# Building half of the MLP's low weight parts with an accumulating DMA instead of a VectorE subtraction

## The chip, the core and the metric

The kernel runs on one NeuronCore of a Trainium2 chip. Five instruction streams matter here: PE (TensorE: matrix products into PSUM), DVE (VectorE), ACT (ScalarE), POOL (GpSimd, here only the issuer of a few DMAs) and SP (SyncE, the issuer of nearly all DMAs). Each stream runs its own instructions in order and waits on semaphores for the others. Transfers between HBM and SBUF are done by 16 DMA engines that serve all queues.

The metric is the device time of one execution in microseconds (us). The kernel before takes 2251.57 us, the median of three runs (2249.9 to 2251.72).

## What is computed

A two-layer decoder trunk over 256 positions with a model width of 2048, in float32. Layer 0 mixes positions with two recurrent head groups, layer 1 with a dilated sliding-window attention. Each layer ends with the same MLP, whose hidden width is 8192:

```python
def squared_relu_mlp(h, w1, w2):
    return jnp.square(jax.nn.relu(h @ w1)) @ w2

def reference(...):
    h = x
    for layer in range(DEPTH):
        hn = rms_norm(h, norm_mix[layer])
        ...
        h = h + mix
        h = h + squared_relu_mlp(rms_norm(h, norm_mlp[layer]), mlp_w1[layer], mlp_w2[layer])
    return rms_norm(h, final_norm)
```

The change touches only the weights `mlp_w1` (2048 x 8192 in each layer) and `mlp_w2` (8192 x 2048 in each layer), which are 256 MB of the kernel's float32 weights.

## The kernel before

**Products from two parts.** The kernel gives PE its operands as `F32R`. Every operand is split into a high part, its value rounded by the cast to that type, and a low part, what the rounding left over: `w = hi + lo`. A product is then the sum of three: high by high, high by low and low by high. The activations are kept split in `bufa` and `bufb`, with the high halves in columns 0 to 255 and the low halves in columns 256 to 511 of each block.

**Weight tiles ("units").** All weights are cut into units of 128 x 2048 values, 1 MB each. They are listed in the order of use in `units`; the MLP's are 256 of them. In each layer four rounds `q` follow one another, each with 16 units of `w1` and then 16 units of `w2`. `unit()` hands out the split unit that is due and calls `fetch()` for one that is due later. `fetch()` takes a buffer `raw` (three exist), issues the load on SP and constructs `Weights`, which splits the unit in two halves of 1024 columns:

- `A.copy(h, w)` at L97: ACT rounds the raw half into `hi`.
- `V.tensor_tensor(l, w, h, subtract)` at L98: DVE writes `lo = raw - hi`.

The pools `whi` and `wlo` hold five half tiles each, so two and a half units. Half number n (counted over all units) therefore takes the place of half n - 5, and can be written only when PE has used that one for the last time.

**How PE uses a unit of `w1`.** `project` with `cross` goes through 16 blocks of 128 columns, and for each issues one product with `hi` (512 columns wide) and one with `lo` (256 wide). The first half tile is free in the middle of the unit and the second at its end. The result goes from PSUM through `folded` (ACT copies at L182, DVE adds at L184), DVE's squared ReLU (L571) and `split_to` (ACT L189, DVE L190) into `bufb`.

**How PE uses a unit of `w2`.** `tokens` goes twice through the unit, once for each half of the positions (`j`), with four blocks `i` of 512 columns each time and three products in a block: (xh, hi), (xh, lo), (xl, hi). Blocks 0 and 1 lie in the first half tile and 2 and 3 in the second. The first half tile is thus free after six of the eight steps and the second after all eight. `add_res` (DVE L536) adds the result to the residual.

**What sets the order.** All products go through `mm`, which chains them in program order. The rest is ordered by a scheduler that sees priorities: weight loading and splitting run ahead (`stream`), and short evacuations further ahead (`urgent`). Once scheduled, the order on each engine is fixed. POOL issues three small DMAs: two tables at the start (L207, L209) and the positions at L596.

Of the kernel before, what the change touches and what calls it, by code (L numbers as in the profile page):

```python
# [10 lines left out]
F32 = mybir.dt.float32  # L11
# [3 lines left out]
AF = mybir.ActivationFunctionType  # L15
OP = mybir.AluOpType
# [24 lines left out]
def trunk_kernel(ctx, tc, x, xtok, cols, tab, masks, pos, fin, w_in, w_gate, w_out, w_qkv, w_o, w1, w2, out):  # L41
    nc = tc.nc
# [13 lines left out]
    V, A, T = nc.vector, nc.scalar, nc.tensor  # L56
# [8 lines left out]
    made = {}  # L65
# [6 lines left out]
    for step in ORDER.split():  # L72
        src, first, n = where[step[0]]
# [9 lines left out]
    at = [0, 0]  # L83

    class Weights:
        def __init__(self, raw, now=True):
            self.raw = raw
            self.hi = [whi.tile([P, 1024], F32R, name="hi") for _ in range(2)]
            self.lo = [wlo.tile([P, 1024], F32R, name="lo") for _ in range(2)]
            if now:  # L90
                self.split(0, 1024)
                self.split(1024, 1024)

        def split(self, at, n):
            h, l = self.part(at, n)
            w = self.raw[:, at:at + n]
            A.copy(h, w)  # L97
            V.tensor_tensor(l, w, h.bitcast(F32), OP.subtract)  # L98

        def part(self, at, n):  # L100
            i, r = divmod(at, 1024)
# [2 lines left out]
    def fetch():  # L104
        u = at[0]
        if u >= len(units):
            return
        at[0] += 1
        src, i = units[u]
        with stream():  # L110
            r = wraw.tile([P, 2048], F32, name="raw")
            nc.sync.dma_start(r, src[i])
            made[u] = Weights(r)

    def fetch_first():
        for u in range(4):
# [18 lines left out]
    def unit(src, i):  # L135
        u = at[1]
        assert units[u][0] is src and units[u][1] == i, (u, i)
        at[1] += 1
        if u + 2 >= at[0]:
            fetch()  # L140
        return made.pop(u)
# [379 lines left out]
    for step in ORDER.split():  # L521
        i = int(step[1])
# [173 lines left out]
    r = tmp.tile([P, 2], F32, name="nr2", bufs=2)  # L696
# [6 lines left out]
    for h in range(2):  # L703
        at = slice(h * 1024, h * 1024 + 1024)
# [111 lines left out]
```

## Time and profile before

The profile shows one execution. Its span, from the first to the last instruction, is 2248.2 us; the same execution took 2250.34 us as timed, so 2.1 us lie around the span. Line numbers are those of the kernel before.

| what | value |
|---|---|
| time, median of three runs | 2251.57 us |
| time of the profiled execution | 2250.34 us |
| its span | 2248.2 us |
| granted TensorE clock, share of full | 0.998 |
| DVE busy | 1411.2 us (63%) |
| ACT busy | 1059.7 us (47%) |
| POOL busy | 1.9 us |
| read from HBM | 410.70 MB |

"Busy" is the time in which an engine executes an instruction. A group of instructions is given as line, engine, operation and tiles, followed by count, total busy time and mean duration. "Idle before" is the time for which the engine stood still just ahead of these instructions, with the one whose semaphore ended it. The DMA share is the mean busy share of the 16 DMA engines. The time of a DMA to landing runs from its issue to the arrival of its last byte's semaphore.

### The profile page before, as it was taken

The page shows a single profiled execution, that of the slowest core. Times are in us where ns is not written, and L with a number is a line of the kernel's source. Part 1 is how long each engine was busy: PE and PEld are TensorE (multiplying, and loading weights), DVE is VectorE, ACT ScalarE, POOL GpSimd, SP SyncE. Part 2 cuts the span into 40 slices and gives each one's busy share as a digit, 9 for nine tenths or more (in the row PEclk, how much of TensorE's full clock was granted, in tenths as well). Part 3 has the DMA queues.
Part 4 walks back from the last instruction along what each step waited for, and adds up shares of the span by engine and source line. Part 5 has one row for each costly group of instructions (what it writes and reads, how often), then busy time and mean ns, then how long its engine had stood idle before and what let it go on. Part 6 is the DMA issues. An engine that isn't in the chain of part 4 may idle for free.

```text
span 2248.2 us, 30488 instructions
## 1 busy us (share of the span) xinstructions
PE 2228.6 (99%) x12196; PEld 1930.5 (86%) x12196; DVE 1411.2 (63%) x2212; ACT 1059.7 (47%) x1537; POOL 1.9 (0%) x7
## 2 busy tenths in 40 slices
PE   9999999999999999999999999999999999999997
PEld 8999998888888888888888888888888888888886
DVE  7777896565565565565567878556655655655654
ACT  6444585444344344344545445454434444434443
POOL 0000000000000000000000000000000000000000
PEclk9999999999999999999999999999999999999999
DMA  8444445555555555555554554555555555555553
GB/s 307 151 161 160 150 167 190 187 188 187 199 185 182 201 187 187 187 190 185 187 189 168 171 185 169 187 186 181 178 198 193 188 187 191 185 188 204 188 185 114
DMA packets 58717, 414.51 MB, mean 184 GB/s; under 512 B 6528, under 2 KB 7296, under 8 KB 9168
## 3 DMA queue, kind: packets, MB, share of 16 engines
q1 hardware_dynamic: 58320, 412.20, 52.0%
q8 instruction: 95, 1.56, 0.3%
q0 software_dynamic: 256, 0.38, 0.1%
q14 instruction: 46, 0.38, 0.0%
HBM read 410.70 MB, written 2.10 MB: 184 GB/s over the span
## 4 chain that ended last, share of the span: by engine, by line
PE 97%; ACT 1%; DVE 1%; issue 0%; DMA 0%; SPq 0%; ACTq 0%; DVEq 0%
PE p L146 94%; PE pl L423 1%; PE pl L548 0%; ACT hi L97 0%; PE pl L646 0%; DMA raw<-in_w_in 0%; PE po L667 0%; PE pd L659 0%; DVE bufa L193 0%; ACT L158 0%; DVE lo L98 0%; PE pd L407 0%; PE pl L645 0%; ACT gi L158 0%; PE po L668 0%
## 5 line engine op out<-in xcount | busy, mean ns | idle before, releaser
L98 DVE TENSOR_TENSOR lo<-raw,hi 128x1024 fp32r<-128x1024 f32 (+1 forms) x774 | 945.0, 1221 | 733.4 <-ACT hi L97 717.2
L97 ACT CAST hi<-raw 128x1024 fp32r<-128x1024 f32 (+1 forms) x774 | 811.2, 1049 | 1004.3 <-PE p L146 809.7
L146 PE MATMUL p<-bufa,hi 128*128 128x512 f32 (+1 forms) x3840 | 1147.2, 361 | 2.6 <-DVE bufa L193 2.6
L146 PE MATMUL p<-bufa,lo 128*128 128x256 f32 x3200 | 902.4, 282 | 0.0
L146 PE MATMUL p<-hi,bufb 128*128 128x512 f32 x2560 | 793.7, 390 | 0.0
L146 PEld LDWEIGHTS p<-bufa,hi 128*128 128x128 f32 x3840 | 681.4, 189 | 119.6 <-DVE bufa L193 3.8
L146 PEld LDWEIGHTS p<-bufa,lo 128*128 128x128 f32 x3200 | 605.8, 189 | 1.1
L146 PEld LDWEIGHTS p<-hi,bufb 128*128 128x128 f32 x2560 | 479.9, 188 | 99.1
L146 PE MATMUL p<-lo,bufb 128*128 128x512 f32 x1280 | 498.2, 389 | 0.0
L146 PEld LDWEIGHTS p<-lo,bufb 128*128 128x128 f32 x1280 | 240.3, 188 | 49.5
L146 PE MATMUL p<-hi,bufa 128*128 128x512 f32 x384 | 123.1, 396 | 0.7 <-ACT hi L97 0.6
L146 PEld LDWEIGHTS p<-hi,bufa 128*128 128x128 f32 x384 | 71.7, 188 | 16.1 <-ACT hi L97 1.6
L146 PE MATMUL p<-lo,bufa 128*128 128x512 f32 x192 | 76.2, 397 | 1.8 <-DVE lo L98 1.8
L189 ACT CAST bufb<-z 128x256 fp32r<-128x256 f32 x136 | 54.3, 399 | 17.4 <-DVE z L571 14.5
L536 DVE SCALAR_TENSOR_TENSOR xall<-p,nm,xall 128x512 f32<-128x512 f32 x64 | 47.9, 748 | 20.1 <-PE p L146 20.1
L190 DVE TENSOR_TENSOR bufb<-z,bufb 128x256 fp32r<-128x256 f32 x136 | 57.0, 419 | 3.8 <-ACT bufb L189 3.8
L571 DVE SCALAR_TENSOR_TENSOR z<-z 128x256 f32<-128x256 f32 x128 | 54.5, 426 | 4.4
L184 DVE TENSOR_TENSOR z<-p,t 128x256 f32<-128x256 f32 x128 | 53.5, 418 | 0.0
L182 ACT COPY t<-p 128x256 f32<-128x256 f32 x128 | 46.9, 366 | 0.0
L247 ACT ACTIVATE z<-xall 128x512 bf16<-128x512 f32 x32 | 20.2, 632 | 55.7 <-DVE xall L536 55.7
L146 PEld LDWEIGHTS p<-lo,bufa 128*128 128x128 f32 x192 | 36.1, 188 | 10.7 <-DVE lo L98 3.7
L423 PE MATMUL pl<-qk 128*128 128x64 f32 x224 | 31.1, 261 | 0.0
(197 smaller groups left out, 730.6 us busy)
## 6 DMA issues: line engine op xcount, KB each, us to landing
raw<-in_w SPq DMA_DIRECT2D x256, 1024.0 KB, 4.8
raw<-in_w_qkv SPq DMA_DIRECT2D x48, 1024.0 KB, 4.8
raw<-in_w_in SPq DMA_DIRECT2D x46, 1024.0 KB, 4.8
raw<-in_w_out SPq DMA_DIRECT2D x16, 1024.0 KB, 4.7
raw<-in_w_o SPq DMA_DIRECT2D x16, 1024.0 KB, 4.8
xall<-in_xtok SPq DMA_DIRECT2D x1, 2048.0 KB, 9.2
raw<-in_w_gate SPq DMA_DIRECT2D x2, 1024.0 KB, 4.8
out<-xall SPq DMA_DIRECT2D x4, 512.0 KB, 4.0
```

The source lines that it names most:

```text
L97: A.copy(h, w)
L98: V.tensor_tensor(l, w, h.bitcast(F32), OP.subtract)
L146: chain[:] = [after(T.matmul(*args, **kw), chain)]
L182: A.copy(t, p[:, S:])
L184: V.tensor_tensor(z, p[:, :S], t, OP.add)
L189: A.copy(dst[:, :S], src)
L190: V.tensor_tensor(dst[:, S:], src, dst[:, :S].bitcast(F32), OP.subtract)
L247: A.activation(q, xres[:, j, n * 512:n * 512 + 512], AF.Square, accum_out=self.ss[:, j, n:n + 1])
L423: T.matmul(pl[:, j], kq[:, js], halves(qp[:, js], c, True), start=True, stop=True)
L536: V.scalar_tensor_tensor(xres[:, j, at], ps[j], 1.0 if scale is None else scale[:, j:j + 1], xres[:, j, at], op0=OP.mult, op1=OP.add)
L571: V.scalar_tensor_tensor(z, z, 0.0, z, op0=OP.max, op1=OP.mult)
```

## The change

Units of the MLP with an odd index no longer use DVE for their low part. ACT writes the negated high part into `lo`, and a DMA issued by POOL then reads the same weights from HBM a second time and adds them onto `lo`, so that `lo = -hi + raw`. Even units, and all units of other weights, keep the subtraction on DVE. In the changed kernel the subtraction stands at L100, the high part at L98, the negation at L102 and the accumulating DMA at L103.

```diff
     class Weights:
-        def __init__(self, raw, now=True):
+        def __init__(self, raw, now=True, again=None):
             self.raw = raw
+            self.again = again
...
             w = self.raw[:, at:at + n]
             A.copy(h, w)
-            V.tensor_tensor(l, w, h.bitcast(F32), OP.subtract)
+            if self.again is None:
+                V.tensor_tensor(l, w, h.bitcast(F32), OP.subtract)
+            else:
+                A.activation(l, h.bitcast(F32), AF.Copy, scale=-1.0)
+                nc.gpsimd.dma_start(l, self.again[:, at:at + n], accum_op=OP.add)
...
             r = wraw.tile([P, 2048], F32, name="raw")
             nc.sync.dma_start(r, src[i])
-            made[u] = Weights(r)
+            made[u] = Weights(r, again=src[i] if src in (w1, w2) and i % 2 else None)
```

There are 128 such units, 64 of `w1` and 64 of `w2`, with two halves each: 256 instructions move from DVE to ACT, and 256 DMAs of 128 x 1024 float32 (512 KB) are new on POOL's queue. The order of PE's instructions stays as it was but for five groups of four transposes (L548), which move ahead by a few products. In the `w1` stage ACT's fixed order for two units becomes: `t`, negation, `bufb`, high part, negation, high part, `t`, high part, `bufb`, high part. In the `w2` stage it is: high part, negation, high part, negation, high part, high part.

## The prediction

> **What bounds the kernel now.** I read the page first: the busy shares and the chain that ended last.
>
> ```profile
> span 2248.2 us, 30488 instructions
> ...
> PE 2228.6 (99%) x12196; PEld 1930.5 (86%) x12196; DVE 1411.2 (63%) x2212; ACT 1059.7 (47%) x1537; POOL 1.9 (0%) x7
> ...
> PE 97%; ACT 1%; DVE 1%; issue 0%; DMA 0%; SPq 0%; ACTq 0%; DVEq 0%
> ```
>
> PE is never without work for long: 19.6 us of 2248.2. The waits of PE alone say who is to blame for what is left.
>
> ```profile
> PE p L146 <- DVE bufa L193: 2.6, 4, 0.9
> PE p L146 <- DVE lo L98: 1.8, 4, 0.8
> PE po L447 <- ACT st L433: 1.3, 1, 1.3
> PE po L202 <- DVE spare L577: 1.1, 1, 1.1
> PE p L146 <- ACT hi L97: 0.6, 1, 0.6
> ```
>
> The columns are total us, times, longest. All DVE waits together are 2.6 + 1.8 + 1.1 = 5.5 us. The low part made by DVE, which the change wants to relieve, holds PE up for 1.8 us in the whole execution. The stretch of layer 0's MLP, taken by itself, has no hole at all (busy us of PE, PEld, DVE, ACT, POOL; then clock, DMA share, GB/s):
>
> ```profile
> 432.75:1074.08 641.33, 641.33 (x3283) 546.08 (x3284) 370.74 (x450) 281.52 (x363) 0.00 (x0) 1.00 0.54 189
> ```
>
> So the MLP runs at PE's pace at full clock, DVE is busy 58% of it, and the DMA engines 54%. The change can win next to nothing. What it can lose depends on whether the new, longer way to `lo` still fits in the lead that the five half tiles give.
>
> **What is removed.** 256 of DVE's 774 subtractions go, and ACT gets as many negations.
>
> ```profile
> L98 DVE TENSOR_TENSOR lo<-raw,hi 128x1024 fp32r<-128x1024 f32 (+1 forms) x774 | 945.0, 1221 | 733.4 <-ACT hi L97 717.2
> ```
>
> DVE loses 256 x 1.221 = 313 us, none of it on the path that sets the end except at most the 1.8 us above. I count nothing for it.
>
> **What is added on ACT.** The nearest rows are the rounding copy of the same size, and an activation and a copy of 128x256.
>
> ```profile
> L97 ACT CAST hi<-raw 128x1024 fp32r<-128x1024 f32 x770 | 808.8, 1051 | 1003.3 <-PE p L146 809.7 <-issue 187.9 <-DVE hz L635 4.7
> L189 ACT CAST bufb<-z 128x256 fp32r<-128x256 f32 x136 | 54.3, 399 | 17.4 <-DVE z L571 14.5 <-DVE z L517 2.8
> L182 ACT COPY t<-p 128x256 f32<-128x256 f32 x128 | 46.9, 366 | 0.0
> ...
> L158 ACT ACTIVATE qk<-hz 128x256 f32<-128x256 f32 x16 | 6.5, 409 | 0.0
> ```
>
> An activation costs 409 - 399 = 10 ns more than a cast, so a negation is 1.06 us and all of them 271 us. ACT then has for two `w1` units 4 x 1.05 + 2 x 1.06 + 2 x (0.40 + 0.37) = 7.9 us. To know what that is out of, the pace of a unit is needed, from ACT's timeline in a `w1` stage:
>
> ```profile
> 860.94 1.05 ACT L97 CAST hi<-raw 128x1024 fp32r<-128x1024 f32 x1 [1.51 <-issue]
> 861.89 0.37 ACT L182 COPY t<-p 128x256 f32<-128x256 f32 x1
> 863.73 1.05 ACT L97 CAST hi<-raw 128x1024 fp32r<-128x1024 f32 x1 [1.47 <-PE p L146]
> 864.68 0.40 ACT L189 CAST bufb<-z 128x256 fp32r<-128x256 f32 x1
> 866.60 1.05 ACT L97 CAST hi<-raw 128x1024 fp32r<-128x1024 f32 x1 [1.51 <-issue]
> ```
>
> From 860.94 to 866.60 a unit takes 5.66 us, two take 11.3, and ACT fills 7.9 of these. Work that queues behind a negation (`t` and `bufb`, for which DVE's ReLU and, after three PSUM buffers, PE wait) comes up to 1.06 us later; three buffers are two units of cover. Where the cover is thin, at the end of a layer with its short chain of ACT and DVE steps, eight groups late by 1.06 us would cost 8.5 us. I count nothing.
>
> **What is added on the way to `lo`.** Before: place free, high part 1.05, subtraction 1.22. Now: place free, high part, negation, DMA, semaphore. Call L the time from the DMA's issue to its landing. How large may L be? In the `w2` stage ACT's timeline shows when places come free:
>
> ```profile
> 1059.43 1.05 ACT L97 CAST hi<-raw 128x1024 fp32r<-128x1024 f32 x1 [3.04 <-PE p L146]
> 1060.78 1.05 ACT L97 CAST hi<-raw 128x1024 fp32r<-128x1024 f32 x1 [0.30 <-PE p L146]
> 1064.87 1.05 ACT L97 CAST hi<-raw 128x1024 fp32r<-128x1024 f32 x1 [3.04 <-PE p L146]
> ```
>
> A `w2` unit takes 1064.87 - 1059.43 = 5.44 us, and the two frees are 1.35 us apart, which is two of the eight steps, as the loop says. The second half of an odd unit takes the place of the first half of the unit two before (n - 5 is 2u + 1 - 5). That one is free at 6/8 of its unit and the new one is needed at 2/8 of its own: 1.5 x 5.44 = 8.16 us, and 0.23 more because a product with `hi` goes first (24 in 5.44 us). Off go 1.05 and 1.06 on ACT and some 0.1 for semaphores: **L may be 6.2 us**. The first half has 2 units, 10.88 us, and so L up to 8.9. In `w1` a first half has 11.3 + 0.24 (two thirds of a block's 5.66 / 16), less 0.95 for the high part until `t` starts (861.89 - 860.94), 0.37 and 1.06: L up to 9.1; the second half has about the same, since `bufb` ahead of it is done by the time its place is free.
>
> And how large is L? No accumulating DMA is in this trace. The rows for DMAs (KB each, median us to landing):
>
> ```profile
> raw<-in_w SPq DMA_DIRECT2D x256, 1024.0 KB, 4.8
> ...
> tab__187<-in_tab POOLq DMA_DIRECT2D x1, 257.0 KB, 3.8
> ...
> ppi<-in_pos POOLq DMA_DIRECT2D x1, 32.0 KB, 2.0
> ```
>
> From 32 KB to 1024 KB it is 2.8 us more, so 2.9 us per MB on top of a fixed 1.9. An accumulation has to read its target as well as its source: 512 KB written need 1024 KB read. One pass over 512 KB would be 1.9 + 1.45 = 3.4 us, two passes 4.8, if the DMA engines are free. They are not: the raw loads fill 54% of them, so in the mean the moving part stretches by 1/(1 - 0.54) = 2.17: one pass 5.0, two passes 1.9 + 2.9 x 2.17 = 8.2. The other bound is the table row: from 32 to 257 KB it takes 1.8 us more, 8.0 us per 1000 KB, from POOL's queue in the crowded start; its fixed part is then 1.7, and two passes at that price are 1.7 + 8.2 = 9.9. **L lies between 3.4 and 9.9. I take 8.2**: the price of the raw loads, which fill the same stretch, with two passes, since a read of the target can't be left out. Then the second half of each odd `w2` unit is 8.2 - 6.2 = 2.0 us late. PE waits for it, frees the places later, and the next round starts as much later: the loss repeats for each of 2 x 4 x 8 = 64 units. In `w1`, 8.2 is below 9.1, but the engines' own time is short there: per two units 2 MB of raw loads and two passes over 1 MB are 4 x 2.9 = 11.6 us, in 11.3. That is 0.3 us for each of 64 pairs. (In `w2` the same 11.6 fits in 10.9 + 2.0.)
>
> The row of the raw loads says nothing of a second operand. The Trainium skill, Collectives: The Full Stack, "The bandwidth ceiling: the fold count and why AG ≠ RS ≠ AR", says that an adding DMA runs at about half the rate of a copy (measured 1.93) because it needs two source reads. By that factor L would be about 8.0 us, 1 MB of accumulation 5.6, and the time an estimated 2250 + 64 x 1.8 + 64 x 0.1 = 2372 us; by the bare row with one pass L is 5.0, and the time unchanged. No run so far shows which holds.
>
> **What is queued on POOL.** The 256 DMAs stand behind the positions' DMA, which waits for layer 0's mixers, and in order among themselves.
>
> ```profile
> POOL ppi L596 <- PE po L449: 297.8, 1, 297.8
> ```
>
> That wait ends about 300 us in, ahead of the first MLP unit, so it delays nothing. SP's loads of `raw` start no later than before: an odd unit's `raw` is free after ACT alone.
>
> **The sum.** 64 x 2.0 + 64 x 0.3 = 147 us on the profiled execution's own 2250.3: 2397. Against the median (2251.57) it would be 2399; I state 2397.
>
> **The rivals.**
>
> *Hidden, no slower.* The raw load and the accumulation fall in different parts of a unit's time, so that they hardly share: L is 4.8 to 6.2, below the limit in both stages. For it: the DMA engines idle 46% of the MLP, and `w2`'s limit is missed by only 2.0. Against it: the sharing has to be avoided 64 times. The time stays at 2250, with the DVE waits gone 2244.8 at best. It decides from L below 6.2. The Trainium skill, DMA: Bandwidth & Descriptors, "Anatomy of one DMA — SWDGE (gpsimd) path", gives about 2.0 us plus the bytes at 436 GB/s for a DMA from POOL's queue; that estimate is 3.2 us for one pass and 4.4 for two, which lands here.
>
> *The DMA engines become the bound.* If 1 MB of accumulation costs over 7.1 us (a late `w2` pair, 10.9 + 2.0, less 5.8 of raw loads), every pair of units, in `w1` and in `w2`, takes what the DMA engines take. At the table row's 8.2 us per MB in one pass a pair is 5.8 + 8.2 = 14.0, so 64 x (2.7 + 3.1) = 371 us more: 2621; in two passes 22.2, and 3671. For it: that row is the only large one from POOL's queue, and the price of the adding itself is unknown. Against it: the table was loaded among the crowded first loads.
>
> *DVE holds POOL up.* If POOL can't write a DMA's descriptors while DVE works, each waits up to one subtraction, 1.22 us. L is 9.4, `w2` loses 3.2 x 64 = 205, `w1` 0.3 x 64 = 19: 2474. Against it: DVE's instructions become fewer. The Trainium skill, SBUF — State Buffer, "Who interferes with whom", says that a DVE instruction in a two-port mode shuts GpSimd out for its whole length, and that a `tensor_tensor` has no such mode and gets in the way of GpSimd's reads only; no run so far shows either.
>
> *Only ACT's delay shows.* L fits, and the ends of the layers cost the 8.5 us of above: 2259.
>
> **How the numbers follow.** The forecast, late low parts in `w2`, with L from just over 6.2 to some 9.5 (3.3 x 64 + 0.4 x 64 = 237, so 2256 to about 2490): 0.45. DMA engines as the bound: 0.28. Hidden: 0.17. DVE holding POOL: 0.05. ACT's delay alone: 0.05. A measurement of this kernel tells 0.2%, 4.5 us, from no change: three runs lie within 1.8 us. Of the hidden case 0.03 is faster and 0.14 the same; all others are slower, 0.83. The range runs from 2249, which takes in the hidden case, to 2850: half of the DMA-bound case lies above it (0.14) and the 0.03 below, so 0.83 is inside. The forecast's own range is 2256 to 2490.
>
> **What would show it.** The accumulating DMAs' row with about 8 us to landing; PE's waits in `w2`, on products with `lo`, of about 2 us at each odd unit, and of some 0.3 us in `w1`; DMA share in the MLP of 0.9 and more; the negation at 1.06 us. If PE waits in `w1` as long as in `w2` and the DMA share is near 1, the DMA engines are the bound. If PE has no new wait, L is below 6.2 and the forecast is wrong.

## The result, and the profile after

| | before | changed |
|---|---|---|
| time, median | 2251.49 us (four runs, 2249.9 to 2251.72) | 2417.94 us (four runs, 2402.99 to 2434.6) |
| ratio | | 1.0743, 95% interval 1.0704 to 1.0782 |
| span of the profiled execution | 2248.2 us | 2401.2 us |
| mean granted TensorE clock | 0.998 | 0.992 |

The kernel became 7.4% slower; 2397 us had been forecast. The profiled execution is the fastest of the four. The page of the changed kernel, its busy shares, the DMA engines' share by slices, POOL's DMA queue, the chain that ended last and the DMA issues:

```profile
PE 2269.8 (95%) x12196; PEld 1935.6 (81%) x12196; DVE 1114.3 (46%) x1956; ACT 1320.8 (55%) x1793; POOL 222.7 (9%) x263
...
DMA  8444455999999999999855454579999989999996
...
q0 software_dynamic: 37120, 134.61, 31.4%
...
PE 51%; DMA 30%; issue 17%; ACT 1%; POOL 1%; DVE 0%; POOLq 0%; SPq 0%; ACTq 0%; DVEq 0%
...
raw<-in_w SPq DMA_DIRECT2D x256, 1024.0 KB, 6.6
lo<-in_w POOLq DMA_DIRECT2D x256, 512.0 KB, 7.6
```

The two MLP stretches stand out in the DMA row: where the engines were half busy they are now at nine tenths and more. The new DMAs on POOL's queue took 31.4% of all engines' time, 754 us for 128 MB, so 5.9 us per MB written. The chain that ended last, 97% PE before, now leads for 30% through DMAs, nearly all of them these. DVE lost 297 us of busy time and ACT gained 261; in the chain ACT has 1%, as before, and DVE nothing.

PE's waits, and the groups of its products with `lo` (busy us and mean ns, then idle time just before and what ended it):

```profile
PE p L151 <- DMA lo<-in_w: 111.3, 95, 3.2
PE p L151 <- DVE bufa L198: 2.5, 4, 0.8
PE p L151 <- DVE lo L100: 1.6, 3, 0.8
```

```profile
L151 PE MATMUL p<-bufa,lo 128*128 128x256 f32 x3200 | 907.7, 284 | 26.4 <-DMA lo<-in_w 25.6
...
L151 PE MATMUL p<-lo,bufb 128*128 128x512 f32 x1280 | 511.4, 400 | 85.8 <-DMA lo<-in_w 85.7
...
L103 POOL DMA_DIRECT2D lo<-in_w x256 | 220.7, 862 | 1858.5 <-ACT lo L102 1824.6
...
L102 ACT ACTIVATE lo<-hi 128x1024 fp32r<-128x1024 f32 x256 | 271.3, 1060 | 6.0
```

One wait is new and it is the accumulating DMA: 25.6 us of it ahead of `w1`'s products (in from `bufa`), 85.7 ahead of `w2`'s (in from `bufb`). The other two rows are nearly as they were. The old wait for DVE's low part was 1.8 us; it went down to 1.6, which is all that relieving DVE brought.

Here is one such wait, from the timelines of POOL and PE in a `w2` stage:

```profile
966.18 0.86 POOL L103 DMA_DIRECT2D lo<-in_w  x1 [5.94 <-ACT lo L102]
971.10 0.86 POOL L103 DMA_DIRECT2D lo<-in_w  x1 [4.06 <-ACT lo L102]
```

```profile
976.39 0.61 PE L151 MATMUL p<-hi,bufb 128*128 128x512 f32 x2
979.04 0.50 PE L151 MATMUL p<-lo,bufb 128*128 128x512 f32 x1 [2.04 <-DMA lo<-in_w]
979.38 0.72 PE L151 MATMUL p<-hi,bufb 128*128 128x512 f32 x2
979.90 0.63 PE L151 MATMUL p<-lo,bufb 128*128 128x512 f32 x1
980.33 1.05 PE L151 MATMUL p<-hi,bufb 128*128 128x512 f32 x2
```

The second half's DMA is issued at 971.10. PE has done the products with `hi` at about 977.0 and starts the first with `lo` at 979.04, 7.9 us after the issue. Then something happens that was not in the forecast: a product with `lo` takes 0.63 us instead of 0.39. The stretches around it show why (busy us of PE, PEld, DVE, ACT, POOL; then granted clock, DMA share, GB/s):

```profile
820.00:912.00 92.00, 89.43 (x498) 76.16 (x497) 36.80 (x62) 58.27 (x78) 13.78 (x16) 1.00 1.00 266
912.00:1010.00 98.00, 90.10 (x383) 71.88 (x382) 25.01 (x26) 50.15 (x49) 13.62 (x16) 0.98 0.94 253
976.00:979.80 3.80, 1.76 (x8) 1.17 (x7) 0.41 (x1) 1.57 (x2) 0.87 (x1) 1.00 0.90 237
979.80:983.20 3.40, 3.40 (x9) 2.63 (x9) 0.75 (x1) 0.00 (x0) 0.00 (x0) 0.50 1.03 235
983.20:987.00 3.80, 3.80 (x18) 3.09 (x18) 1.18 (x2) 3.05 (x3) 0.86 (x1) 1.00 0.45 111
```

The first row is a `w1` stage with the DMA engines fully busy, the second the `w2` stage behind it. The third holds the wait, and in the 3.4 us after it the granted clock is 0.50. There are nine such stretches of 3.4 us in this execution's MLPs, none before. They are the step from 0.998 to 0.992 in the mean clock: 0.006 x 2401 = 14 us. The other executions of the changed kernel had 0.990, 0.985 and 0.983, and the four times rise as the clock falls, from 2402.99 to 2434.6 us. So the clock's part differs from run to run and is larger in the median than in the profile.

### The profile page after: what moved, and what is told of

The parts are those of the page before. It is cut to its first block, busy times and chain, and to the rows that moved or that the text cites. A ratio compares the mean times of both kernels' runs of the same rounds, so it can differ in the third digit from the quotient of the medians.

```text
span 2401.2 us, 31090 instructions
## 1 busy us (share of the span) xinstructions
PE 2269.8 (95%) x12196; PEld 1935.6 (81%) x12196; DVE 1114.3 (46%) x1956; ACT 1320.8 (55%) x1793; POOL 222.7 (9%) x263
## 3 DMA queue, kind: packets, MB, share of 16 engines
q0 software_dynamic: 37120, 134.61, 31.4%
## 4 chain that ended last, share of the span: by engine, by line
PE 51%; DMA 30%; issue 17%; ACT 1%; POOL 1%; DVE 0%; POOLq 0%; SPq 0%; ACTq 0%; DVEq 0%
PE p L151 48%; DMA lo<-in_w 29%; POOL lo L103 1%; PE pl L428 1%; ACT hi L98 0%; PE pl L553 0%; PE pl L651 0%; DMA xall<-in_x 0%; PE po L672 0%; PE pd L664 0%; ACT L163 0%; PE pd L412 0%; PE pl L650 0%; ACT gi L163 0%; PE po L673 0%
## 5 line engine op out<-in xcount | busy, mean ns | idle before, releaser
L98 ACT CAST hi<-raw 128x1024 fp32r<-128x1024 f32 (+1 forms) x774 | 810.0, 1047 | 891.1 <-PE p L151 873.0
L100 DVE TENSOR_TENSOR lo<-raw,hi 128x1024 fp32r<-128x1024 f32 (+1 forms) x518 | 631.1, 1219 | 876.8 <-ACT hi L98 871.9
L151 PE MATMUL p<-bufa,lo 128*128 128x256 f32 x3200 | 907.7, 284 | 26.4 <-DMA lo<-in_w 25.6
L151 PE MATMUL p<-hi,bufb 128*128 128x512 f32 x2560 | 803.4, 394 | 0.0
L151 PE MATMUL p<-lo,bufb 128*128 128x512 f32 x1280 | 511.4, 400 | 85.8 <-DMA lo<-in_w 85.7
L151 PEld LDWEIGHTS p<-hi,bufb 128*128 128x128 f32 x2560 | 486.1, 190 | 100.6
L103 POOL DMA_DIRECT2D lo<-in_w x256 | 220.7, 862 | 1858.5 <-ACT lo L102 1824.6
L102 ACT ACTIVATE lo<-hi 128x1024 fp32r<-128x1024 f32 x256 | 271.3, 1060 | 6.0
```

The lines of the kernel that those rows point to most:

```text
L102: A.activation(l, h.bitcast(F32), AF.Copy, scale=-1.0)
L103: nc.gpsimd.dma_start(l, self.again[:, at:at + n], accum_op=OP.add)
L151: chain[:] = [after(T.matmul(*args, **kw), chain)]
```

## The experiments

The theory after the result: the accumulation costs the DMA engines about twice what a copy of as many bytes costs, lands later for it, and PE waits wherever the time to landing is above what the place's lead allows: 6.2 us for a second half in `w2`, about 9 elsewhere. The rivals were ACT's negations, the second read from HBM, POOL's path, and DMA time alone without any lead. Every experiment is an edit of the changed kernel, except one of the kernel before. Times are medians, each beside its own runs of the kernel before (2251.56 to 2251.64 us).

**The DMA copies and does not add** (`x1_copy`).

```diff
-                nc.gpsimd.dma_start(l, self.again[:, at:at + n], accum_op=OP.add)
+                nc.gpsimd.dma_start(l, self.again[:, at:at + n])
```

> The DMA from GpSimd stays, with its wait for the negation and its second read of the weights, but it overwrites lo and does not add (lo = raw, so the output is not the reference's). Theory (the second operand doubles the DMA engines' time: a 4096-byte piece of the accumulation takes 328 ns, a plain one about 160): time to landing falls from 7.6 to about 5 us, below w2's limit of 6.2, and the kernel takes 2250 to 2262 us. Rival (the second read from HBM, or GpSimd's path, costs the time whatever the DMA does): no change, 2390 to 2430 us.

2302.47 us, ratio 1.0228 (1.0209 to 1.0246). The time lies in neither range: two thirds of the loss go, but not all. The price did fall. The page's queue row and issue row of this run:

```profile
q0 software_dynamic: 37120, 134.61, 19.1%
...
lo<-in_w POOLq DMA_DIRECT2D x256, 512.0 KB, 5.8
```

19.1% of 2296.6 us is 439 us for 128 MB, 3.4 us per MB against 5.9. A piece of 4096 bytes takes 174 ns in the median of the packet records and 328 with the addition. But in `w2` the second halves still landed 6.4 us after issue in the mean, just over the limit of 6.2, with single ones up to 8.6; PE waited 36.7 us for them, and 0.2 in `w1`. So the addition is most of the price, and `w2`'s lead is short even for a copy.

**Only the negation** (`x2_neg_only`).

```diff
-                nc.gpsimd.dma_start(l, self.again[:, at:at + n], accum_op=OP.add)
```

> The negation stays on ACT, the accumulating DMA is left out (lo = -hi, so the output is not the reference's). Theory (ACT's 256 negations are covered): 2249 to 2256 us. Rival (work behind the negations on ACT, t and bufb, comes late and holds PE up): 2270 us or more.

2249.71 us, ratio 0.9993 (0.9984 to 1.0003). ACT's 271 us are covered, and taking half of the MLP's subtractions from DVE gains nothing that can be measured. Neither of the change's engine terms can be seen in the time.

**More lead in `w2`** (`x3_by_k`), and the kernel before in the same order (`x5_before_by_k`).

```diff
-                ps = tokens(w2, layer * 64 + q * 16 + 4 * n, bufb)
+                ps = tokens(w2, layer * 64 + q * 16 + 4 * n, bufb, by_k=True)
```

> The changed kernel, but w2's products go block by block with both halves of the positions in each (i outer, j inner), so that the first half tile is free after 4 of 8 steps and the second is needed at 4 of 8: the second half's lead grows from 1.5 to 2 units, and its limit on the time to landing from 6.2 to about 8.7 us. Theory (w2 loses because the accumulation lands after its limit): w2's loss of about 91 us goes nearly, w1's of about 43 stays: 2290 to 2330 us. Rival (the DMA engines' total time is what w2 lacks): 2390 us or more, as lead does not help there.

> The kernel before, with w2's products block by block as in the run with the changed order. Theory (that order costs nothing by itself, so that what it gave with the change is the lead): 2249 to 2256 us. Rival (it costs part of the 88 us that were left there): 2270 us or more.

The changed kernel takes 2340.3 us in this order (1.0391, 1.0376 to 1.0407), the kernel before 2252.42 (1.0003, 0.9993 to 1.0012). The order is free by itself, and half a unit more lead gives back 78 us; the time is 10 us above the range of the theory. PE still waits for the accumulating DMAs, 25.9 us in `w1` and 39.8 in `w2`:

```profile
PE p L151 <- DMA lo<-in_w: 65.7, 76, 2.6
```

What limits the rest can be read in 400 us of layer 0's MLP; first the run with the new order, then the changed kernel itself:

```profile
600.00:1000.00 400.00, 379.60 (x1888) 315.99 (x1887) 134.95 (x184) 233.76 (x270) 58.46 (x68) 1.00 1.00 267
```

```profile
600.00:1000.00 400.00, 376.07 (x1842) 310.84 (x1841) 130.91 (x178) 225.19 (x262) 56.87 (x66) 0.99 0.97 260
```

With the longer lead the DMA share is 1.00 over both stages, which points to the DMA engines' time as a second limit behind the first. The run with half as many accumulations in this order, further down, is in line with that: it loses 17 us where this one loses 89.

**The weights from SBUF** (`x4_from_raw`).

```diff
-                nc.gpsimd.dma_start(l, self.again[:, at:at + n], accum_op=OP.add)
+                nc.gpsimd.dma_start(l, w, accum_op=OP.add)
```

> The accumulating DMA reads the weights from the raw tile in SBUF and not a second time from HBM. HBM traffic falls back to about 411 MB, the DMA engines move as many bytes as with the change. Theory (DMA engine time and landing against the lead): 2370 to 2440 us, a piece of 4096 bytes still near 328 ns. Rival (HBM's share is what is lacking): 2250 to 2290 us.

2564.89 us, 1.1394 (1.1375 to 1.1413): slower still, and outside both ranges. HBM traffic fell to 410.70 MB and the piece stayed at 328 ns, so the price of a piece doesn't come from the second read of HBM. PE waited 217.2 us for these DMAs, and the granted clock was 0.972. What else is different shows in SP's waits, where the longest is new:

```profile
SPq L117 <- DMA lo<-raw: 1585.3, 157, 14.0
SPq L117 <- DVE lo L100: 311.0, 59, 9.0
```

The raw tile now stays in use until the accumulation has landed, and SP's next load, which needs that place, waits for it. Whether this lengthened loop is the whole of the extra loss wasn't tried.

**Both remedies** (`x6_by_k_copy`): the copy, and `w2` block by block.

> The changed kernel with both: w2 block by block, and the DMA from GpSimd overwriting lo instead of adding (the output is not the reference's). Theory (the loss is the second operand's DMA time and w2's short lead, and nothing else): copies land in 5 to 7 us, below the limits of 8.7 and 9.1, and the kernel takes 2249 to 2260 us. Rival (GpSimd's descriptors or the second read from HBM cost time by themselves): about 2300 us, as with the copy alone.

2251.18 us, 0.9999 (0.9989 to 1.0009), and PE doesn't wait for these DMAs at all. The same 256 DMAs from POOL, with the same second read of 128 MB, cost nothing once they neither add nor have the short lead. That rules out POOL's descriptors and HBM as costs of their own here.

**One stage alone** (`x7_w1_only`, `x8_w2_only`): the condition `src in (w1, w2)` becomes `src is w1` or `src is w2`.

> Only odd units of w1 take the new way, those of w2 go back to DVE. Theory (w1 loses by DMA engine time, 43 us, w2 by its lead, 110 us, each by itself): 2285 to 2300 us. Rival (both stages lose alike, half the loss each): 2325 to 2340 us.

> Only odd units of w2 take the new way, those of w1 go back to DVE. Theory: 2345 to 2370 us. Rival (both stages lose alike): 2325 to 2340 us.

`w1` alone: 2296.7 us (1.0203, 1.0183 to 1.0223), as expected. `w2` alone: 2394.69 us (1.0634, 1.0618 to 1.065), 25 us above the range. So `w2` is the dearer stage, and the losses don't add: 45 + 143 is 188, with both 166. PE's waits of the run with `w2` alone:

```profile
PE p L151 <- DMA lo<-in_w: 99.8, 62, 4.0
```

That is 99.8 us against 85.7 of the full change's `w2`. The clock doesn't clearly differ: it was 0.985 to 0.988 in the four executions with `w2` alone and 0.983 to 0.992 in those of the full change. Why the waits are longer when `w1` has none was not settled.

**One half of each `w2` unit** (`x9_w2_first_half`, `x10_w2_second_half`), the plainest test of the lead: as many DMAs and bytes in both. The edit for the first halves is shown; for the second ones it is `not at`.

```diff
-            if self.again is None:
+            if self.again is None or at:
...
-            made[u] = Weights(r, again=src[i] if src in (w1, w2) and i % 2 else None)
+            made[u] = Weights(r, again=src[i] if src is w2 and i % 2 else None)
```

> Only the first half of each odd unit of w2 takes the new way (64 DMAs), the second half stays on DVE. Theory (the limit is the lead of the place, 8.9 us for a first half; its landing was 6.9 us in the mean with the whole change): next to nothing is late, 2249 to 2262 us. Rival (any accumulation in w2 costs, in proportion to its number): half of the 143 us of w2 alone, about 2320 us.

> Only the second half of each odd unit of w2 takes the new way (64 DMAs as well, as many bytes). Theory (its limit is 6.2 us): with less traffic it lands in 6 to 7.5 us, so 64 units late by 0.3 to 1.3 us each and some clock: 2270 to 2340 us, clearly more than the first half alone. Rival (in proportion to the number): as the first half alone.

First halves: 2251.54 us (1.0001, 0.9991 to 1.0011). Second halves: 2316.36 us (1.0284, 1.026 to 1.0307). The issue rows, first halves first:

```profile
lo<-in_w POOLq DMA_DIRECT2D x64, 512.0 KB, 6.3
```

```profile
lo<-in_w POOLq DMA_DIRECT2D x64, 512.0 KB, 6.5
```

The two land alike, after 6.3 and 6.5 us. The one has 8.9 us, and PE never waits; the other has 6.2, and PE waits 40.8 us for it:

```profile
PE p L151 <- DMA lo<-in_w: 40.8, 55, 2.1
```

These 64 accumulations cost nothing where the lead covers them.

**Every fourth unit** (`x11_quarter`), and the same with `w2` block by block (`x12_by_k_quarter`): `i % 2` becomes `i % 4 == 3`.

> Every fourth MLP unit takes the new way instead of every second (128 DMAs, both stages). Theory: w1 has DMA time to spare and loses nothing; in w2 the second half still lands after 6.2 us (6.4 to 7.5), for 32 units: 2265 to 2310 us. Rival (the total DMA time is all that counts, 5.0 us of loads and 2.6 of accumulation in 11 us): no loss, 2249 to 2256 us.

> Every fourth MLP unit, and w2 block by block (limit about 8.7 us instead of 6.2). Theory (what was left at 2340 us with that order is the DMA engines' total time): with half of the accumulations the landings fall below 8.7 and the kernel takes 2249 to 2258 us. Rival (each accumulation costs some lead whatever the traffic): about half of the 88 us, 2295 us.

With half of the DMAs 2381.49 us (1.0579, 1.056 to 1.0597): a clear miss, since nearly 80% of the loss remains. With the longer lead 2268.91 us (1.0081, 1.0065 to 1.0097), 11 us over the range; PE's waits for the DMAs are 8.5 of its 17 us, and the rest was not settled. The two runs have the same DMAs and differ in the lead alone, so DMA time alone doesn't explain the first. The first run's waits, POOL timeline and 400 us of its MLP:

```profile
PE p L151 <- DMA lo<-in_w: 87.5, 32, 3.7
```

```profile
914.79 0.87 POOL L103 DMA_DIRECT2D lo<-in_w  x1 [18.91 <-ACT lo L102]
918.82 0.86 POOL L103 DMA_DIRECT2D lo<-in_w  x1 [3.17 <-ACT lo L102]
```

```profile
600.00:1000.00 400.00, 377.59 (x1833) 315.54 (x1832) 166.94 (x210) 192.04 (x230) 29.32 (x34) 0.97 0.73 215
```

PE waits 32 times in `w2`, 87.5 / 32 = 2.7 us each. The second halves land 8.5 us after issue in the mean, though the DMA engines are only 73% busy; second halves alone, without first ones, landed after 6.7. The second DMA is issued 4.0 us after the first, which takes 6.7 us to land, so the two overlap. In the changed kernel they are issued 5.6 us apart in the mean and the second lands after 7.45. So it is what else is in flight in these microseconds that goes with the landing, not the mean share. And the clock costs more here than with twice as many: 0.982, so 0.016 x 2382 = 38 us. The 87.5 and the 38 make up 126 of the 134 us by which the profiled spans differ.

**The limit against the waits.** For each DMA the time to landing was worked out from its issue and landing records and averaged by stage and half. The late part of the mean, times the number of units, against PE's waits for these DMAs:

| run | second half of | landed, us | limit, us | late x units | PE waited, us |
|---|---|---|---|---|---|
| changed kernel | `w2` | 7.45 | 6.2 | 1.25 x 64 = 80 | 85.7 |
| changed kernel | `w1` | 9.33 | 9.1 | 0.23 x 64 = 15 | 25.6 |
| `w2` alone | `w2` | 7.66 | 6.2 | 1.46 x 64 = 93 | 99.8 |
| `w1` alone | `w1` | 9.46 | 9.1 | 0.36 x 64 = 23 | 27.6 |
| second halves only | `w2` | 6.69 | 6.2 | 0.49 x 64 = 31 | 40.8 |
| every fourth | `w2` | 8.54 | 6.2 | 2.34 x 32 = 75 | 87.5 |
| copy | `w2` | 6.38 | 6.2 | 0.18 x 64 = 12 | 36.7 |
| full change, block by block | `w2` | 9.51 | 8.7 | 0.81 x 64 = 52 | 39.8 |
| full change, block by block | `w1` | 9.43 | 9.1 | 0.33 x 64 = 21 | 25.9 |
| every fourth, block by block | `w2` | 8.68 | 8.7 | 0 | 8.1 |
| copy, block by block | `w2` | 6.82 | 8.7 | 0 | 0 |

The limits are those of the loop's steps, worked out before any of these runs. The product comes out low where single DMAs are late in a mean that is near the limit: of the copy's 64 second halves in `w2`, 36 land after more than 6.2 us, and their late parts add up to 33. One row, `w2` block by block, comes out too high; why was not settled. The run from SBUF is left out, since its first halves are late as well.

The trace also gives the limit itself: the time to landing, less what PE waited. For the second halves of `w2` that PE waited for this is 5.87 us nearly every time, in the changed kernel, with second halves alone and with every fourth unit. Only the first odd unit of a `w2` stage has more, 7.3 to 7.5 us in the runs with `w2` alone, because the place that it takes is still one of `w1`'s. So 6.2 was 0.3 us too long, and the short lead is that of seven of the eight odd units of a stage.

## Why the prediction was right

*PE bounds, nothing to gain.* Right: the negation alone, with half of the MLP's subtractions gone, measures 0.9993 (0.9984 to 1.0003).

*The negation.* 1.06 us forecast, 1060 ns measured, covered as said.

*The limit of L.* 6.2 us for the second half of a `w2` unit; 5.87 as read from the waits. That the lead decides is shown by the two halves apart: landing after 6.3 us is free with a lead of two units, and after 6.5 it costs 65 us with one and a half.

*The price.* Two passes at the raw loads' price, 2.9 us each per MB, so 5.8; measured 5.9. Against the copy from the same queue the addition is a factor of 1.89 by the pieces' medians (328 and 174 ns) and of 1.72 by the queue's whole time (754 and 439 us). The Trainium skill, Collectives: The Full Stack, "The bandwidth ceiling: the fold count and why AG ≠ RS ≠ AR", has the adding step of a reduce-scatter run at about half the rate of a copy (1.93 measured), because the add needs two source reads; the pieces agree.

*L.* 8.2 us forecast; 7.6 measured as the median, and 7.45 in the mean for the halves that decide. Size near, way of getting there wrong: I stretched the moving part by the mean DMA share. The run with every fourth unit has a smaller share than the full change (0.73 against 0.97) and its second halves land later (8.54 against 7.45). The neighbours in time decide, the first half's accumulation and the raw loads; which of them weighs more was not separated. That the mean share gave nearly the right number for this one spacing is luck.

*The sum.* `w2`: 128 us forecast. PE waited 85.7 there, and the clock took most of its 14. `w1`: 19 forecast; PE waited 25.6, and the time between the first and the last ReLU of a round of 16 grew from 84.6 to 89.9 us in the mean, 0.35 us for a unit or 45 us in all. The term of `w1` was less than half of what it measured: L for all DMAs was put at 8.2, below its limit of 9.1, but its second halves land after 9.3. Whether that or the engines' full time (share 1.00) holds `w1` up was not separated. `w2`'s term was somewhat large. The two errors nearly cancel: the profiled spans differ by 153 us, against 147 forecast. So the waits and their place were foreseen, and that the number is so close is in part luck; the median, with its lower clock, is 21 us above the forecast.

Of the 153 us, 112 are idle time of PE (2401.2 - 2269.8, against 19.6 before) and 41 are longer busy time. The clock explains 14 of the 41. The rest goes with the waits. PE's products overlap: in a `w2` unit they start 0.23 us apart (24 in 5.44) and last 0.39 each. A wait leaves the last 0.16 us of the product before it uncovered, and the first product behind it takes 0.50. That is 0.27 us for a wait, so an estimated 26 for the 95 waits. The copy's run fits as well: 33 waits would be 9 us and its clock 2, and PE is busy 11 us longer than before.

*What was left out.* The clock, 14 us here and 38 in the run with every fourth unit, and the 0.27 us that a wait adds to the busy time. A wait of PE costs more than its length.

*The rivals.* Hidden is wrong in both stages. DVE holding POOL has no support: the same DMAs as copies, with the longer lead, cost nothing beside the same DVE. The DMA engines as the bound turned out to be the second limit, right behind: the share is 1.00 in the `w1` stage shown, and in both stages once `w2` has more lead. ACT's delay alone is wrong: the negations by themselves cost nothing.

## What to carry to other kernels

An accumulating DMA in place of an engine's subtraction is free only if the new way's full length, with the DMA's time to landing under local traffic, fits the lead that the buffers give; work that lead out for each half of each tile from the loop's steps, since here half a unit of lead decided between nothing and 65 us. Price an accumulation as two copies of its bytes and add it to the loads of the same stretch before asking about latency. And don't relieve an engine that isn't late: DVE had 42% to spare in layer 0's MLP, and its relief was worth nothing.

## What the runs showed of the hardware

- An accumulating DMA from HBM onto SBUF takes 328 ns (median) for a piece of 4096 bytes, a plain one from the same queue 174. With the weights read from SBUF it is 328 as well.
- Issuing one keeps POOL busy for 862 ns in the changed kernel's row; the copy's instruction takes 528 ns.
- A short wait of PE can halve the granted clock for 3.4 us: ahead of the stretch shown PE waited 2.04 us. The Trainium skill, TensorE: Matmul & The Clock Gate, "Part 1: The HAM clock gate (the "warmup" mystery)", has the clock fall to half after an idle window of about 3.4 us and rise after as long a busy one. The length of the slow stretch agrees; the idle time that brought it on was shorter here, and PE's longest wait for these DMAs in the changed kernel was 3.2 us.
- What decided was how much of one fixed piece of time PE stood still. All nine slow stretches start on one grid of 3.41 us. In the piece of the grid just ahead of each, PE was idle for 1.99 us or more; in no other piece of that execution for more than 1.75. With every fourth unit the two figures are 1.90 and 1.87, with `w2` alone they overlap (1.82 and 1.92). So about 1.9 us of 3.41 is the border that these traces show.
- Hence fewer waits can cost more clock if each is longer: with every fourth unit 30 of PE's 32 waits for these DMAs are of 1.9 us or more, in the changed kernel 20 of 95. The clock was 0.980 to 0.985 in the four executions of the first and 0.983 to 0.992 in those of the second.
